# Even mixer: sixteen heads in two groups with one division each, weight splitting off GpSimd, the second group's keys moved behind three heads

## The chip, the core and the metric

The kernel runs on one core of one Trainium2 chip. The metric is the device time of one execution in microseconds (us), the median of several. The core has TensorE (PE, matrix products; the loading of its stationary side is shown as PEld), VectorE (DVE), ScalarE (ACT), GpSimd (POOL) and SyncE (SP), which here only issues DMAs. Each engine works through a queue of its own in a fixed order and waits on semaphores of the others.

## The reference

A decoder of two blocks on 256 tokens of width 1024 in fp32. The stages are, in order: a feed-forward layer, the even mixer, two feed-forward layers, the odd mixer, a feed-forward layer, and then the second block's mixer and feed-forward layer. The change lies in the even mixer, which computes

```python
proj = h @ w_in                                   # 1024 -> 1536
qa, ka, va, qb, kb, vb = split(proj)              # 8 + 2 + 2 heads of 64, twice
qa = apply_axial_rope(rms_norm(qa, q_gain)); ka = apply_axial_rope(rms_norm(ka, k_gain))
oa = softmax(qa ka^T / 8) va                      # 8 query heads, 2 key heads, all 256 keys
qb, kb = apply_rope(qb), apply_rope(kb)
ob = softmax with sink(qb kb^T / 8, |q - k| <= 128) vb
return concatenate([oa, ob]) @ w_out
```

## The kernel before, in words

Activations lie with the features on the 128 partitions. Weights are streamed from memory in blocks of 128 x 1024 (`load_unit`, line 254, five buffers) and split into a rounded part wh and a rest wl: `prep` (line 277) makes wh on ACT (line 288) and wl on DVE or, for the blocks that `ON_POOL` (line 117) names, on GpSimd (line 290). `block` (line 294) hands out the next block and first prepares all up to LOOK = 6 blocks ahead; wh and wl have five buffers each.

The program is traced once. A scheduler then fixes the order of each engine's queue from a model of the times: an instruction that was written earlier goes first, one that is ready may be put ahead of one that is not. Buffers come from pools by tag: NSLOT common slots of 128 x 1024, and for temporaries of 512 columns the tag c2 with seven buffers (`tmp`, line 232), which w2, p and pT share. PSUM has four banks mm, two sc for scores and two aux for transposes.

`mix0` (line 636) is the even mixer. FIRST is the windowed group of eight heads (b = 1), SECOND the global one (b = 0). The program goes:

1. `proj(kv)` (line 748): four weight blocks, PE lines 341 to 343, read out by ACT with the row scale of the norm (line 660).
2. `k_in(FIRST)`: rotation of the first group's keys (`rot`, line 678): a product t (line 687, mostly on GpSimd), two multiplies on DVE (line 693) and a sum (line 695).
3. `proj(q[FIRST])`, `q_in(FIRST)`: the queries and their rotation. `k_T(FIRST)`: transposes on PE (line 701) and copies to kp.
4. `k_in(SECOND)`: squares on GpSimd (line 667), sums on DVE (line 668), an inverse root (`rsqrt`, line 431: three ACT and four GpSimd steps), scaling (line 675), rotation. Then `q_T(FIRST)`, four transposes, and `k_T(SECOND)`, which clears the halves of kT on GpSimd (line 560) and splits the transposed keys (lines 553, 554).
5. `proj(q[SECOND])`, `q_in(SECOND)`.
6. Heads one after the other (`attention`, line 610): scores (lines 567 or 569), maximum with the mask on DVE (line 779), exponential with its sum on ACT (line 577), the sink's term (line 786), reciprocal (line 584) and scaling of p by it (line 587, one half on GpSimd, one on DVE); two heads later the transposes of p (line 594) and the copy pT (line 596); three heads later, for each pair of heads, the products with v (line 603, v loaded, pT moving, 256 columns) and the split into oh and ol (`split_tile`, line 606). Between the heads of FIRST stand the four `q_T(SECOND)` (lines 543, 544).
7. `out_half` 0 (line 1452) takes the four pairs of FIRST and is interleaved with the heads of SECOND step by step; `out_half` 1 follows.

The rows also show lines of the last mixer, `mix2`: its E tiles (line 1161), and the products of its softmax heads, with pT loaded and v moving, and their division (lines 1287 to 1300).

Of the kernel before, what the change touches and what calls it, by code (L numbers as in the profile page):

```python
# [10 lines left out]
F32R = mybir.dt.float32r  # L11
# [4 lines left out]
P = 128  # L16
T = 256
# [5 lines left out]
NSLOT = 23  # L23
# [93 lines left out]
ON_POOL = {"ffn2": (6, 16, 3), "mix0": (0, 20, 3), "mix1": (0, 32, 4)}  # L117
# [93 lines left out]
class K:  # L211
    def __init__(self, tc, ctx, aps, stages):
        self.tc, self.nc, self.aps, self.ctx = tc, tc.nc, aps, ctx
        pool = lambda n, b, **k: ctx.enter_context(tc.tile_pool(name=n, bufs=b, **k))
        self.cp = pool("const", 1)
        self.wp = pool("wp", 1)
        self.sp = pool("slots", 1)
        self.tp = pool("tmp", 1)
        self.ap_ = pool("att", 1)
        self.dp = pool("dram", 1, space=bass.MemoryType.DRAM)  # L220
        self.pp = pool("ps", 1, space=bass.MemoryType.PSUM)
        self.nblk = sum(STAGE_NBLK[s] for s in stages)
        self.raw, self.ready = {}, {}
        self.start = {s: sum(STAGE_NBLK[r] for r in stages[:i]) for i, s in enumerate(stages)}
        self.next_unit = self.next_prep = self.cur = 0
        self.n6 = 5

# [66 lines left out]
    def block(self):  # L294
        b = self.cur
        self.cur += 1
        while self.next_prep < min(self.nblk, b + LOOK):
            self.prep()
        return self.ready.pop(b)
# [336 lines left out]
    def mix0(self, next_gain):  # L636
# [25 lines left out]
        def rms(src, h, tagn, scale):  # L662

            ss = self.tmp("ss" + tagn, 2 * h, 1)
            for tt in range(2):
                sq = self.tmp("w2", 512, 2)[:, :h * 64]
                nc.gpsimd.tensor_tensor(out=sq, in0=src[:, tt], in1=src[:, tt], op=ALU.mult)
                nc.vector.tensor_reduce(out=ss[:, tt * h:(tt + 1) * h],
                                        in_=sq.rearrange("p (h d) -> p h d", d=64), axis=AX.X, op=ALU.add)
# [8 lines left out]
        def rot(src, dst, h, n, sub):  # L678

            for tt in range(2):  # L680
# [5 lines left out]
                e = nc.vector if (tt, n, h) == (1, 2, 8) else nc.gpsimd  # L686
                e.tensor_tensor(out=t3, in0=v, in1=C.unsqueeze(1).to_broadcast([P, h, 64]), op=ALU.mult)
# [21 lines left out]
        kT = [self.slot("kT", F32R).rearrange("p (n c) -> p n c", n=4)]  # L709
# [3 lines left out]
        self.zero_others(kp)  # L713
        qT = lambda b, t: qs[2 * b + t // 2][:, t % 2]
# [16 lines left out]
        def k_T(b):  # L731
            if b == FIRST:
                ps = tr(kr[:, b], 0)
                for h in range(2):
                    own = slice(64 * h, 64 * h + 64)
                    nc.scalar.activation(kp[own, h], ps[own], AF.Copy)
            else:
                self.zero_others(kT[b][:, 2:4])
                self.split_k(kT[b][:, 0:2], kT[b][:, 2:4], tr(kr[:, b], 0))
# [15 lines left out]
        k_in(SECOND)  # L755
        for t in range(4):
            q_T(FIRST, t)
        k_T(SECOND)
# [5 lines left out]

        def soft_a(i, ps):
            nm, den, mx = [self.tmp(n, 2, 3) for n in ("nm", "den", "mx")]
            r = rq[0][:, i:16:8]
            nc.vector.tensor_reduce(out=mx, in_=ps, axis=AX.X, op=ALU.max)
            nc.vector.scalar_tensor_tensor(out=nm, in0=mx, scalar=-1.0, in1=r, op0=ALU.mult, op1=ALU.mult)
            p = self.head_exp(ps, nm, den, [r[:, 0:1], r[:, 1:2]])  # L770
            self.head_norm(p, den)
            return p

        def soft_b(i, ps):
            nm, den = self.tmp("nm", 2, 3), self.tmp("den", 2, 3)
            mx, es = self.tmp("mx", 2, 3), self.tmp("es", 2, 3)
            s = ps
            for qt in range(2):
                nc.vector.tensor_tensor_reduce(out=s[:, qt], in0=ps[:, qt], in1=band[:, qt], scale=1.0,
                                               scalar=-3e38, op0=ALU.add, op1=ALU.max,  # L780
                                               accum_out=mx[:, qt:qt + 1])
            h = i
            nc.vector.tensor_scalar(out=nm, in0=mx, scalar1=-1.0, scalar2=nsink[:, h:h + 1],
                                    op0=ALU.mult, op1=ALU.min)
            p = self.head_exp(s, nm, den)
            nc.scalar.activation(es, nm, AF.Exp, bias=sink[:, h:h + 1])
            nc.vector.tensor_tensor(out=den, in0=den, in1=es, op=ALU.add)
            self.head_norm(p, den)
            return p

        def head(b, t, half):
            c = 128 + 256 * b + 64 * half
            v = [kv[:, kt, c:c + 64] for kt in range(2)]
            j = t if b == FIRST else 4 + t
            if b == FIRST:
                return lambda: (qp[:, t], kp, None, v, j, half)
            return lambda: (qT(b, t), kT[b][:, 0:2], kT[b][:, 2:4], v, j, half)

        def soft(i, ps):
            return (soft_b if (FIRST if i < 8 else SECOND) else soft_a)(i % 8, ps)  # L800

        hs = [head(b, t, half) for b in (FIRST, SECOND) for t in range(4) for half in range(2)]
        done = []
        att = self.attention(hs, soft, OH, OL, done)
        for _ in proj(q[SECOND]):
            pass
        q_in(SECOND)
# [719 lines left out]
```

## Time and profile before

| | |
|---|---|
| median of 3 runs | 1379.62 us (1379.5 to 1379.85) |
| the profiled execution | 1380.82 us, of which its span, first to last instruction, is 1379.0 |
| PE busy | 1327.5 us (96%) |
| DVE, ACT, GpSimd busy | 1012.8, 807.6 and 308.1 us |
| mean granted TensorE clock | 0.982 of 2.4 GHz |
| HBM read | 228.96 MB |
| even mixer | about 203.8 to 312.4 us of the span |

A granted clock of 1.00 means 2.4 GHz and one of 0.50 means 1.2 GHz. Matmuls are pipelined: a record is longer than the distance to the next one, so what a matmul costs is read from the starts of a series. An fp32 matmul that is not in the rounded form stands as two records. Idle time of an engine stands in brackets ahead of the instruction that ended it, with the one that released it.

### The profile page before, as it was taken

What the parts mean: (1) busy time and instruction counts of PE and PEld (TensorE: products, weight loads), DVE (VectorE), ACT (ScalarE), POOL (GpSimd) and SP (SyncE); (2) the same over time, 40 slices, a digit from 0 to 9 for tenths busy, and PEclk for the clock granted to TensorE, in tenths of its full rate; (3) what the DMA queues carried; (4) which work ended last, traced back from release to release, by engine and by line L of the source; (5) the groups of instructions that cost most, each with busy time, mean ns of one, the idle gap of its engine ahead of it and who ended that gap; (6) DMA issues with size and microseconds to landing.
All of it is one profiled execution on the core that took longest, in us unless ns stands there. A gap on an engine that the chain in (4) does not pass through costs nothing.

```text
span 1379.0 us, 22443 instructions
## 1 busy us (share of the span) xinstructions
PE 1327.5 (96%) x8150; PEld 1166.1 (85%) x8150; DVE 1012.8 (73%) x1841; ACT 807.6 (59%) x1496; POOL 308.1 (22%) x355
## 2 busy tenths in 40 slices
PE   6999999699999999999999999999999998999997
PEld 5888887488888888888899888888877888899987
DVE  7877666868776768776659878777767768787754
ACT  4655545656655446555468756555566546676642
POOL 4000146432000210001434340001243124641101
PEclk9999999899999999999999999999999998899999
DMA  7555555025555555555565345555545304265561
GB/s 255 184 184 189 190 196 173 32 77 183 185 192 189 183 177 191 190 192 183 184 229 193 113 167 185 183 190 192 184 141 186 118 33 152 92 199 181 184 216 47
DMA packets 64255, 231.48 MB, mean 168 GB/s; under 512 B 7240, under 2 KB 7376, under 8 KB 64144
## 3 DMA queue, kind: packets, MB, share of 16 engines
q1 hardware_dynamic: 61632, 221.41, 48.1%
q0 software_dynamic: 2512, 8.64, 1.8%
q8 instruction: 64, 1.05, 0.3%
q14 instruction: 47, 0.39, 0.1%
HBM read 228.96 MB, written 1.06 MB: 167 GB/s over the span
## 4 chain that ended last, share of the span: by engine, by line
PE 90%; DVE 6%; ACT 2%; issue 1%; DMA 0%; POOL 0%; DVEq 0%; SPq 0%; ACTq 0%
PE mm L308 25%; PE mm L306 14%; PE sc L308 7%; PE mm L312 5%; PE mm L313 5%; PE mm L314 5%; PE sc L306 4%; PE mm L343 4%; PE mm L341 4%; PE mm L342 4%; PE mm L305 3%; PE mm L603 2%; DVE wl L290 1%; PE sc L313 1%; PE sc L314 1%
## 5 line engine op out<-in xcount | busy, mean ns | idle before, releaser
L290 DVE TENSOR_TENSOR wl<-raw,wh 128x1024 fp32r<-128x1024 f32 (+1 forms) x406 | 502.4, 1240 | 267.7 <-ACT wh L288 266.5
L288 ACT ACTIVATE wh<-raw 128x1024 fp32r<-128x1024 f32 (+1 forms) x425 | 443.4, 1045 | 435.5 <-issue 201.8
L308 PE MATMUL mm<-xs,wh 128*128 128x512 f32 x826 | 297.7, 400 | 3.2 <-DVE xs L410 3.2
L306 PE MATMUL mm<-xs,wl 128*128 128x256 f32 x944 | 245.5, 281 | 0.0
L308 PE MATMUL mm<-h,wh 128*128 128x512 f32 x672 | 237.9, 398 | 0.0
L306 PE MATMUL mm<-h,wl 128*128 128x256 f32 x704 | 191.5, 280 | 0.0
L306 PEld LDWEIGHTS mm<-xs,wl 128*128 128x128 f32 x944 | 179.7, 190 | 10.6
L308 PEld LDWEIGHTS mm<-xs,wh 128*128 128x128 f32 x826 | 155.8, 189 | 36.9 <-DVE xs L410 5.4
L413 POOL TENSOR_TENSOR sq<-xt 128x256 f32<-128x256 f32 x48 | 41.1, 859 | 513.1 <-DVE xt L527 483.5
L308 PEld LDWEIGHTS mm<-h,wh 128*128 128x128 f32 x672 | 126.0, 188 | 29.2
L308 PE MATMUL sc<-xs,wh 128*128 128x512 f32 x406 | 144.8, 396 | 0.0
L306 PEld LDWEIGHTS mm<-h,wl 128*128 128x128 f32 x704 | 132.9, 189 | 3.1
L306 PE MATMUL sc<-xs,wl 128*128 128x256 f32 x464 | 120.1, 279 | 0.0
L312 PE MATMUL mm<-xs,wh 128*128 128x256 f32 x384 | 110.5, 289 | 1.0 <-ACT wh L288 0.8
L313 PE MATMUL mm<-xs,wh 128*128 128x256 f32 x384 | 110.2, 287 | 0.1
L314 PE MATMUL mm<-xs,wl 128*128 128x256 f32 x384 | 109.6, 286 | 0.3 <-DVE wl L290 0.3
L306 PEld LDWEIGHTS sc<-xs,wl 128*128 128x128 f32 x464 | 87.5, 188 | 5.1
L308 PEld LDWEIGHTS sc<-xs,wh 128*128 128x128 f32 x406 | 76.1, 188 | 15.5
L312 PEld LDWEIGHTS mm<-xs,wh 128*128 128x128 f32 x384 | 73.8, 193 | 3.6 <-issue 1.5
L313 PEld LDWEIGHTS mm<-xs,wh 128*128 128x128 f32 x384 | 74.0, 193 | 1.6 <-issue 0.8
L314 PEld LDWEIGHTS mm<-xs,wl 128*128 128x128 f32 x384 | 74.0, 193 | 1.3 <-issue 0.7
L343 PE MATMUL mm<-wh,xs 128*128 128x512 f32 x144 | 56.6, 397 | 1.6 <-DVE xs L959 1.6
(376 smaller groups left out, 2683.0 us busy)
## 6 DMA issues: line engine op xcount, KB each, us to landing
raw<-wst SPq DMA_DIRECT2D x417, 512.0 KB, 3.3
m1b<-m1bias POOLq DMA_DIRECT2D x8, 512.0 KB, 4.8
xt<-xT SPq DMA_DIRECT2D x4, 256.0 KB, 5.1
patf<-m2pat POOLq DMA_DIRECT2D x2, 512.0 KB, 6.5
kb<-scr POOLq DMA_DIRECT2D x2, 512.0 KB, 4.5
out<-x2n SPq DMA_DIRECT2D x4, 256.0 KB, 2.0
raw<-wst SPq DMA_DIRECT2D x2, 256.0 KB, 4.3
m0tab<-m0tab POOLq DMA_DIRECT2D x1, 512.0 KB, 4.6
```

The lines of the kernel that those rows point to most:

```text
L288: self.nc.scalar.activation(wh[:, c], r[:, c], AF.Copy)
L290: e.tensor_tensor(out=wl[:, c], in0=r[:, c], in1=wh[:, c].bitcast(F32), op=ALU.subtract)
L305: mm(ps, wh, x2, start=True, stop=False)
L306: mm(ps[:, :T], wl, x2[:, :T], start=False, stop=False, skip_group_check=True)
L308: mm(ps, wh, x2, start=False, stop=last)
L312: mm(ps, wh, xh, start=first, stop=False)
L313: mm(ps, wh, xl, start=False, stop=False)
L314: mm(ps, wl, xh, start=False, stop=last)
L341: mm(ps, xh, wh, start=first, stop=False)
L342: mm(ps, xh, wl, start=False, stop=False)
L343: mm(ps, xl, wh, start=False, stop=last)
L413: nc.gpsimd.tensor_tensor(out=sq, in0=self.x(j), in1=self.x(j), op=ALU.mult)
```

## The change

Weight blocks of this mixer are split by DVE alone. The squares of the rms norm go to ACT, the product t of every rotation to DVE. The second group's keys are prepared behind the first three heads of the first group instead of ahead of all heads, and the look-ahead of the weights is set to 1 while the second group's queries are projected. Each group of eight heads is one generator, `group`: it keeps the sums of all its heads in den, multiplies unscaled p with v in such a way that pT is loaded and v moves (64 columns), gathers all eight heads in two PSUM banks with the tokens on the partitions, divides once, transposes the result in four pieces and splits it. The second group's heads come from a second call, interleaved with the first output half as before. The rests of the split keys get a tile of their own, kT becomes a c2 temporary, a slot o holds each group's result, and NSLOT falls from 23 to 22.

```diff
-NSLOT = 23
+NSLOT = 22
-ON_POOL = {"ffn2": (6, 16, 3), "mix0": (0, 20, 3), "mix1": (0, 32, 4)}
+ON_POOL = {"ffn2": (6, 16, 3), "mix1": (0, 32, 4)}
...
-        while self.next_prep < min(self.nblk, b + LOOK):
+        while self.next_prep < min(self.nblk, b + self.look):
...
-                nc.gpsimd.tensor_tensor(out=sq, in0=src[:, tt], in1=src[:, tt], op=ALU.mult)
+                nc.scalar.activation(sq, src[:, tt], AF.Square)
...
-                e = nc.vector if (tt, n, h) == (1, 2, 8) else nc.gpsimd
-                e.tensor_tensor(out=t3, in0=v, in1=C.unsqueeze(1).to_broadcast([P, h, 64]), op=ALU.mult)
+                nc.vector.tensor_tensor(out=t3, in0=v, in1=C.unsqueeze(1).to_broadcast([P, h, 64]), op=ALU.mult)
...
-        kT = [self.slot("kT", F32R).rearrange("p (n c) -> p n c", n=4)]
+        kT = self.tmp("kT", 2 * T, dt=F32R).rearrange("p (n c) -> p n c", n=2)
...
+        kl = self.ap_.tile([P, 2, T], F32R, tag="klo", name="kl", bufs=1)
+        self.zero_others(kl)
...
-                self.zero_others(kT[b][:, 2:4])
-                self.split_k(kT[b][:, 0:2], kT[b][:, 2:4], tr(kr[:, b], 0))
+                self.split_k(kT, kl, tr(kr[:, b], 0))
...
         k_T(FIRST)
-        k_in(SECOND)
         for t in range(4):
             q_T(FIRST, t)
-        k_T(SECOND)
...
+        def group(b):
+            st = {}
+            po = [self.mm_ps().rearrange("p (h d) -> p h d", h=8) for _ in range(2)]
+            for i in range(8 + 3):
+                if i < 8:
...
+                    scale = (soft_b if b else soft_a)(i, ps)
+                    p = self.tmp("p", 2 * T).rearrange("p (a b) -> p a b", a=2)
+                    for qt in range(2):
+                        nc.scalar.activation(p[:, qt], ps[:, qt], AF.Exp, bias=nm[:, b, qt, i:i + 1],
+                                             scale=scale[qt] if scale else 1.0,
+                                             accum_out=den[:, b, qt, i:i + 1])
+                    st[i] = p
+                yield
+                j = i - 2
+                if 0 <= j < 8:
+                    st[j] = self.head_T(st[j])
+                j = i - 3
+                if 0 <= j < 8:
+                    pT = st.pop(j)
+                    c = 128 + 256 * b + 64 * (j % 2)
+                    for tt in range(2):
+                        for kt in range(2):
+                            nc.tensor.matmul(po[tt][:, j], pT[:, kt, tt * P:(tt + 1) * P], kv[:, kt, c:c + 64],
+                                             start=kt == 0, stop=kt == 1)
+                yield
...
+            rd = self.tmp("grd", 16, 2).rearrange("p (t h) -> p t h", t=2)
+            nc.vector.reciprocal(rd, d)
+            o = self.slot("o").rearrange("p (t c) -> p t c", t=2)
+            for tt in range(2):
+                nc.vector.tensor_tensor(out=o[:, tt].rearrange("p (h d) -> p h d", h=8), in0=po[tt], op=ALU.mult,
+                                        in1=rd[:, tt].unsqueeze(2).to_broadcast([P, 8, 64]))
+            for t in range(4):
+                j = t if b == FIRST else 4 + t
+                self.split_tile(OH(j), OL(j), tr(o, t * P))
+                yield
+
+        att = group(FIRST)
+        self.look = 1
         for _ in proj(q[SECOND]):
             pass
+        self.look = LOOK
+        for _ in range(6):
+            next(att)
+        k_in(SECOND)
+        k_T(SECOND)
         q_in(SECOND)
-        for _ in range(4):
-            next(att)
-        n = 0
-        while len(done) < 4:
+        for n, _ in enumerate(att):
             if n % 2 == 0 and n < 8:
                 q_T(SECOND, n // 2)
-            next(att)
-            n += 1
-        self.interleave(self.out_half(OH, OL, 0, None), att)
+        self.interleave(self.out_half(OH, OL, 0, None), group(SECOND))
```

## Rows read from the trace of the kernel before

**Rows 1.** Busy time of each engine by stretch of the even mixer (start and end in us, length, then busy us and number of instructions of PE, PE's weight loads, DVE, ACT and GpSimd, the granted clock of TensorE, the DMA share and GB/s). The first sum is that of 204 to 237.7, the last that of 237.9 to 312.4:

```profile
sum 33.70, PE 33.70 PEld 27.76 DVE 21.01 ACT 18.79 POOL 20.86; mean PE 11.23 PEld 9.25 DVE 7.00 ACT 6.26 POOL 6.95
...
243.20:256.80 13.60, 5.67 (x16) 4.01 (x17) 12.96 (x41) 6.50 (x24) 4.72 (x8) 0.50 0.15 49
...
sum 74.40, PE 61.94 PEld 48.30 DVE 57.28 ACT 46.00 POOL 33.24; mean PE 12.39 PEld 9.66 DVE 11.46 ACT 9.20 POOL 6.65
```

**Rows 2.** The chain of waits that set the end, the piece that holds the keys' rotation (start, us on the chain, what):

```profile
237.49 8.14 DVE kr L693 x4
```

**Rows 3.** The two kinds of multiply of line 693, by source line: shortest, median and longest in ns, first and last start in us:

```profile
L693 DVE TENSOR_TENSOR kr<-kv,m0g x8: 210/216/7814, 217.7 to 245.4; 128x64 f32<-128x64 f32 x8
L693 DVE TENSOR_TENSOR qr<-q,m0g x8: 408/412/1520, 226.3 to 248.8; 128x256 f32<-128x256 f32 x8
```

**Rows 4.** Timeline of GpSimd, 226 to 246 (start, us, line, operation; in brackets the idle time before it and what ended it):

```profile
226.36 1.54 POOL L687 TENSOR_TENSOR w<-q,m0g 128x512 f32<-128x512 f32 x1 [4.71 <-ACT q L660]
...
230.40 1.65 POOL L667 TENSOR_TENSOR w<-kv 128x128 f32<-128x128 f32 x2
...
237.66 0.87 POOL L687 TENSOR_TENSOR w<-kv,m0g 128x128 f32<-128x128 f32 x2
...
242.79 2.48 POOL L687 TENSOR_TENSOR w<-q,m0g 128x512 f32<-128x512 f32 x2
```

**Rows 5.** Timeline of PE, 236 to 272:

```profile
237.95 1.89 PE L567 MATMUL sc<-kp,qp 128*128 128x256 f32 x8
...
245.97 0.66 PE L701 MATMUL aux<-ident,kr 128*128 128x128 f32 x2 [5.92 <-DVE kr L695]
251.43 2.08 PE L567 MATMUL sc<-kp,qp 128*128 128x256 f32 x4 [4.80 <-ACT p L577]
...
258.77 0.66 PE L594 MATMUL aux<-ident,p 128*128 128x128 f32 x4
```

**Rows 6.** Timelines of GpSimd (the two DMA issues) and of ACT (the first write of the last xs slot):

```profile
16.52 0.59 POOL L268 DMA_DIRECT2D m0row<-m0row  x1
...
199.37 0.49 ACT L409 ACTIVATE xs<-xt,cols 128x256 fp32r<-128x256 f32 x1
...
199.78 0.58 POOL L268 DMA_DIRECT2D m0tab<-m0tab  x1
```

**Rows 7.** Timeline of DVE, 213 to 237.5:

```profile
217.65 1.18 DVE L693 TENSOR_TENSOR kr<-kv,m0g 128x64 f32<-128x64 f32 x4
218.75 0.48 DVE L695 TENSOR_TENSOR kr<-kr,w 128x128 f32<-128x128 f32 x2
...
232.70 0.69 DVE L695 TENSOR_TENSOR qr<-qr,w 128x512 f32<-128x512 f32 x1
...
234.45 0.47 DVE L668 TENSOR_REDUCE ssk<-w 128x2 f32<-128x128 f32 x2
...
236.99 0.49 DVE L675 TENSOR_TENSOR kv<-kv,rrk 128x128 f32<-128x128 f32 x2 [0.94 <-POOL rrk L442]
```

**Rows 8.** Groups of instructions from 200 to 320, shapes kept apart (count, busy us, mean ns, idle before):

```profile
L290 DVE TENSOR_TENSOR wl<-raw,wh 128x1024 fp32r<-128x1024 f32 x17 | 21.7, 1274 | 14.5 <-ACT wh L288 14.4
...
L577 ACT ACTIVATE p<-sc,nm 128x256 f32<-128x256 f32 x16 | 7.4, 468 | 3.4 <-DVE nm L783 2.9 <-DVE rd L584 0.5
...
L779 DVE CUSTOM_DVE_ANT_0 sc<-sc,m0tab 128x256 f32<-128x256 f32 x16 | 6.8, 423 | 0.6 <-PE sc L567 0.5
...
L544 DVE SCALAR_TENSOR_TENSOR qT<-aux,qT 64x256 fp32r<-64x256 f32 x8 | 3.4, 422 | 0.3
...
L779 DVE DVE_READ_ACCUMULATOR2_ANT mx<- 128x1 f32 x16 | 2.1, 134 | 0.0
...
L783 DVE TENSOR_SCALAR nm<-mx,nsink 128x2 f32<-128x2 f32 x8 | 1.8, 221 | 0.1
...
L668 DVE TENSOR_REDUCE ssq<-w 128x8 f32<-128x512 f32 x2 | 1.3, 668 | 0.0
```

**Rows 9.** Timeline of ACT in the last mixer, the second E tile of the third head and the last copy of the second head:

```profile
1092.79 1.08 ACT L1161 ACTIVATE E<-mm 128x512 f32<-128x512 f32 x2 [0.80 <-PE mm L1160]
...
1099.51 0.28 ACT L1198 ACTIVATE A<-aux 128x128 f32<-128x128 f32 x1 [1.23 <-PE aux L1197]
```

**Rows 10.** The chain of waits for the pairs' products (line 603) of today; timeline of PE for the same kind of product in the last mixer; by source line, DVE's division there:

```profile
297.29 1.01 PE mm L603 x6
...
298.89 0.57 PE mm L603 x2
...
1101.69 0.33 PE L1287 MATMUL mm<-va,pT 128*128 128x64 f32 x2
...
1102.29 0.48 PE L1159 MATMUL mm<-patr,lh 128*128 128x512 f32 x1
...
L1300 DVE TENSOR_TENSOR mix<-mm,frd x4: 414/416/425, 1112.0 to 1125.7; 128x256 f32<-128x256 f32 x4
```

**Rows 11.** Busy time by stretch, around two places where PE idles (columns as in rows 1):

```profile
993.00:1000.90 7.90, 5.37 (x41) 4.83 (x39) 4.50 (x8) 3.73 (x6) 1.59 (x2) 1.00 0.44 151
1000.90:1007.70 6.80, 6.80 (x33) 6.80 (x34) 2.35 (x4) 3.04 (x9) 1.39 (x7) 0.50 0.23 77
1018.00:1024.00 6.00, 4.40 (x23) 2.45 (x22) 6.00 (x8) 5.64 (x11) 6.00 (x7) 1.00 0.27 87
```

More of the change, by code (lines that the diff above doesn't have):

```diff
@@ L763, in mix0 @@
         OL = lambda t: ol[t // 4][:, (t % 4) * T:(t % 4 + 1) * T]
+        den, nm = [self.tmp(n, 32, 1).rearrange("p (g t h) -> p g t h", g=2, t=2) for n in ("gden", "gnm")]
         def soft_a(i, ps):
-            nm, den, mx = [self.tmp(n, 2, 3) for n in ("nm", "den", "mx")]
+            mx = self.tmp("mx", 2, 3)
             r = rq[0][:, i:16:8]
             nc.vector.tensor_reduce(out=mx, in_=ps, axis=AX.X, op=ALU.max)
-            nc.vector.scalar_tensor_tensor(out=nm, in0=mx, scalar=-1.0, in1=r, op0=ALU.mult, op1=ALU.mult)
@@ L770, in soft_a @@
-            p = self.head_exp(ps, nm, den, [r[:, 0:1], r[:, 1:2]])
-            self.head_norm(p, den)
-            return p
+            nc.vector.scalar_tensor_tensor(out=nm[:, 0, :, i], in0=mx, scalar=-1.0, in1=r,
+                                           op0=ALU.mult, op1=ALU.mult)
+            return [r[:, 0:1], r[:, 1:2]]
         def soft_b(i, ps):
-            nm, den = self.tmp("nm", 2, 3), self.tmp("den", 2, 3)
-            mx, es = self.tmp("mx", 2, 3), self.tmp("es", 2, 3)
-            s = ps
+            mx = self.tmp("mx", 2, 3)
@@ L778, in soft_b @@
             for qt in range(2):
-                nc.vector.tensor_tensor_reduce(out=s[:, qt], in0=ps[:, qt], in1=band[:, qt], scale=1.0,
+                nc.vector.tensor_tensor_reduce(out=ps[:, qt], in0=ps[:, qt], in1=band[:, qt], scale=1.0,
                                                scalar=-3e38, op0=ALU.add, op1=ALU.max,
                                                accum_out=mx[:, qt:qt + 1])
-            h = i
-            nc.vector.tensor_scalar(out=nm, in0=mx, scalar1=-1.0, scalar2=nsink[:, h:h + 1],
+            nc.vector.tensor_scalar(out=nm[:, 1, :, i], in0=mx, scalar1=-1.0, scalar2=nsink[:, i:i + 1],
@@ L784, in soft_b @@
                                     op0=ALU.mult, op1=ALU.min)
[L785 to L804, printed above, removed]
+            return None
+        def group(b):
[3 more added lines that the diff above has]
+                if i < 8:
+                    t, h = i // 2, i % 2
+                    if b == FIRST:
+                        ps = self.head_scores(qp[:, t], kp, None, h)
+                    else:
+                        ps = self.head_scores(qT(b, t), kT, kl, h)
+                    scale = (soft_b if b else soft_a)(i, ps)
[18 more added lines that the diff above has]
+                yield
+            d = den[:, b]
+            if b:
+                es = self.tmp("es", 16, 1).rearrange("p (t h) -> p t h", t=2)
+                nc.vector.tensor_tensor(out=es, in0=nm[:, b], in1=sink.unsqueeze(1).to_broadcast([P, 2, 8]),
+                                        op=ALU.add)
+                nc.scalar.activation(es, es, AF.Exp)
+                nc.vector.tensor_tensor(out=d, in0=d, in1=es, op=ALU.add)
+            rd = self.tmp("grd", 16, 2).rearrange("p (t h) -> p t h", t=2)
[8 more added lines that the diff above has]
+                yield
@@ L805, in mix0 @@
+        att = group(FIRST)
+        self.look = 1
         for _ in proj(q[SECOND]):
             pass
+        self.look = LOOK
+        for _ in range(6):
+            next(att)
+        k_in(SECOND)
+        k_T(SECOND)
         q_in(SECOND)
-        for _ in range(4):
-            next(att)
-        n = 0
-        while len(done) < 4:
+        for n, _ in enumerate(att):
             if n % 2 == 0 and n < 8:
                 q_T(SECOND, n // 2)
-            next(att)
-            n += 1
-        self.interleave(self.out_half(OH, OL, 0, None), att)
+        self.interleave(self.out_half(OH, OL, 0, None), group(SECOND))
```

## The prediction

> **What bounds the kernel now.** I read the page first: TensorE (PE) is busy for almost the whole span, so a change to the even mixer is worth only what it does to the few places where PE stands still. I then read busy time by stretch for this mixer [rows 1]. While the three projections run, PE has no idle time at all. The attention of the sixteen heads and the output projection take the 74.4 us from 237.9 to 312.4; of these PE is busy for 61.94, so it idles for 12.46. From 243.2 to 256.8 the granted clock is 0.50, the lower level of 1.2 GHz; the 5.67 us of PE work in there would have taken half as long at 2.4 GHz, so 2.8 us more are lost. In all 12.46 + 2.8 = 15.3 us can be won here, and no more, since the work itself stays.
>
> The chain of waits names the cause of the idle time: VectorE's (DVE) rotation of the second group's keys, 8.14 us of the path [rows 2]. By line, one such multiply takes 0.21 us and the worst 7.81 us [rows 3]. GpSimd works without a break from 237.66 to 245.27 on a weight block, the squares and the rotation's products [rows 4], and DVE's instruction ends as that run ends. On PE the keys' transposes come 5.92 us late, and the third head's scores 4.80 us after that [rows 5].
>
> **How the order around it comes about.** Each engine runs a fixed order that the scheduler made: earlier lines first where they are ready. The trace shows a second rule. The load of m0row, which has a buffer of its own, is issued at 16.52; the load of m0tab, which takes one of the common slots, waits until 199.78, right after the last of the four xs slots is first written at 199.37 [rows 6]. So buffers of one tag are given out in the order of their first use in the program. The temporaries of 512 columns (w2, p, pT, and now kT) share one tag too. GpSimd idles 4.71 us before 226.36 and squares the keys of kv at 230.40 only, though DVE rotates the other keys of the same kv from 217.65 [rows 4, 7]: their w2 stands behind that of the queries' rotation. I take it that this order holds for the new code.
>
> **The change part by part.** *Weight blocks off GpSimd, squares to ScalarE (ACT), products to DVE.* This ends the 7.81 us block. Seven weight blocks at 1.27 us, three 512-column products at 0.69 (as a sum of that shape) and four small ones at 0.24 come to DVE, some 12 us [rows 7, 8]. Ahead of 237.9 they are hidden: DVE is busy 21.0 of 33.7 us there, part of it blocked, and PE waits for nothing [rows 1]. If that cover were gone, a weight block would cost its 1.27.
>
> The Trainium skill (SBUF — State Buffer, Who interferes with whom) says that a DVE instruction with two SBUF inputs and a GpSimd one that reads SBUF exclude each other for a whole instruction. Row 7.81 against 0.21 us agrees; by that rule alone the change would give back about 7.6 us, to 1372.0. It says nothing of what is late next; its case is the faster rival below.
>
> *Keys of the second group behind three heads.* What is late next is their own chain. In program order p of heads 0 to 2 and pT of head 0 now take their buffers first, then the squares of the keys, the rotation's products, kT, the squares and products of the queries, and only then p of head 3. Scores start at 238.0. A head costs 0.95 on PE (1.89 for two), 1.25 on DVE (twice 0.42 + 0.13, less their overlap, and 0.22), 0.94 on ACT (two exponentials at 0.47) [rows 5, 8]. With two score banks the third head's scores wait for the first exponentials, 241.2, and its own end near 244.7. From there: two squares, 0.55 (0.28 for an ACT pass of 128x128); reduces 0.47; the inverse root, 2.07 from 234.92 to 236.99; scaling 0.49; rotation 1.58 and two products, 0.5; transposes and the first copy, 0.8: 251.1 [rows 7, 9]. Then the queries: two rotations of a product at 0.69, two multiplies at 0.41 and a sum at 0.69, 4.4 us, and transposes, 0.4: 255.9 at the least [rows 3, 7]. With the reduces (1.3), the keys' low parts (0.84, as the queries' at 0.42 each) and two heads' maxima (2.5) ahead of them on DVE it is 260.5 [rows 8]. I take 256.3, near the lower end, since DVE has waits of the chain in which to do those. Head 1's transposes stand behind these on PE, whose auxiliary banks are also one tag: 256.6. Today head 1's transposes come at 258.77 [rows 5]. In those 18.6 us PE has five heads' scores, one head's transposes (0.5) and products (0.9) and 0.8 of other transposes, 6.95 in all, so it idles 11.7, and the clock falls as it does today, 2.8. **New wait: +14.5**, against the 15.3 removed; bounds +2 (if the chain runs ahead of the heads) to +19. Who waits: all heads from the third on. The five later weight preparations (1.27 on DVE each) fall into this wait and cost nothing; without it they would be 6.4 us on DVE.
>
> *One division per group.* Per head the reciprocal, the sum and the scaling of p go. What PE still waits for them is in the 12.46 already. What is new is a tail after each group: nothing of oh exists before the last head's product. DVE divides two 128x512 pieces (0.42 for 256 columns [rows 10], so about 0.68 each), PE transposes and ACT copies, 0.8 as above; with the handoffs about 2.3 us. Behind the first group two heads' scores of the second (at most the 1.89 of the first group's) cover part, I take 1.3: **+1.0**, between 0 and 2.3. Behind the second group nothing covers it, because the first output half is interleaved one step to one with the heads and runs out before them; before the change the output half takes each pair as it comes. That is 2.3 us of idle PE. What the clock does then is open: after 2.53 us of idle PE between 993 and 1000.9 it was at 0.50 for 6.8 us, which costs 3.4; with 1.60 between 1018 and 1024 it stayed at 1.00 [rows 11]. I take the middle, 1.7: **+4.0**, between 1.5 and 5.7.
>
> [...]
>
> *Products with p as the loaded side.* Eight records for a head now have 128-column loads and 64 moving columns. The same form elsewhere goes at 0.11 each (0.60 for six), 0.88 a head; today a pair takes 1.01 + 0.57, 0.79 a head [rows 10]. Sixteen heads: **+1.4**. *Eight pairs of transposes of the outputs*, 0.25 each, two of them inside the tails: **+1.5**.
>
> *One slot less.* In the last mixer the second E tile of the third head is written at 1092.79 while, by my count of live tiles, all 23 slots are taken; the second head's E is free at about 1099.5 [rows 9]. With 22 that write comes up to 6.7 us later. The third head's work follows the second's on every engine anyway, so I take 0, between 0 and 4, something over half of the 6.7.
>
> **Sum.** -15.3 + 14.5 + 1.0 + 4.0 + 1.4 + 1.5 = +7.1. The profiled execution took 1380.82 (span 1379.0); I put the difference on the median of three runs, 1379.62: **1386.7**.
>
> **The rivals.** *The chain runs ahead of the heads, and it gets faster.* If buffers are not held to program order, DVE and ACT prepare the keys before 237.9. Then the first group is bound by DVE: eight heads at 1.25, the queries' rotation and reduces 5.7, their splitting 8 x 0.42, 19 us from 238 [rows 8], and 3 us behind it to the last product, plus the tail: 262.3. PE has 20.9 us of work in those 24.3, 3.4 idle, no slow clock: -15.3 + 3.4 + 4.0 + 1.4 + 1.5 = -5.0, **1374.6** (1372 to 1377). It decides from the point where head 3's exponentials start before about 250. For it: GpSimd is clear, and scores did move ahead of earlier lines on PE. Against it: the m0tab load and the late squares of the keys.
>
> *The new wait and the savings cancel.* The chain is partly hidden, head 3 starts around 252 and the last tail keeps its clock: the wait comes to +9 and that tail to +2.3, so -15.3 + 9 + 1.0 + 2.3 + 1.4 + 1.5 = -0.1, **1379.5** (1377 to 1382).
>
> *The missing slot bites.* On top of the forecast the third and fourth heads of the last mixer end late, and its output projection with them: up to +4, **1390.7**. Against it: only one tile of one head stands behind the slot.
>
> That the block of DVE goes on by other GpSimd work is no case of its own: only four small steps per inverse root, 0.2 each, remain.
>
> **How the numbers follow.** The forecast with its chain bounds has 0.44, the slot on top 0.08, the cancelling 0.18, the faster rival 0.30. A measurement of this kernel tells apart about 0.2%, 2.8 us: below 1376.9 is faster, above 1382.4 slower. The faster rival gives 0.27 to faster and 0.03 to same; the cancelling one 0.16 to same, 0.01 to each side; the forecast 0.43 to slower and 0.01 to same. So faster 0.28, same 0.20, slower 0.52. The range goes from the middle of the faster rival, 1374, to the upper bound of the chain and the slot, 1392; the likeliest case alone is 1382 to 1391.
>
> **What would show it.** Right: no DVE multiply over 1 us; head 3's exponentials near 254 or later, ACT's squares of the keys after the third head's exponentials; PE idle some 11 us between 245 and 257 at a clock of 0.50; a PE gap of about 2 us just before the second output half. Wrong: squares of the keys before 238, or the first group's last product before 266. The forecast falls with the chain: each microsecond that it is hidden takes one from the sum.

## The result, and the profile after

The changed kernel takes 1389.9 us (median of four runs, 1388.7 to 1391.4), the kernel before 1379.7 beside it: ratio 1.0072, interval 1.006 to 1.0084, slower by 10.2 us. The forecast was 1386.7 in a range of 1374 to 1392. The profiled execution after takes 1389.73, span 1388.0; the span before is 1379.0, so the two traces differ by 9.0.

Where do these 9.0 us come from? First the even mixer of the kernel after in four stretches (columns as in [rows 1]; the first begins with the first scores, the last ends with the first matmul of the next feed-forward layer):

```profile
237.22:251.44 14.22, 6.98 (x38) 5.44 (x36) 10.35 (x43) 7.07 (x24) 0.79 (x4) 1.00 0.23 76
251.44:265.10 13.66, 9.29 (x33) 7.06 (x32) 8.37 (x22) 8.06 (x24) 0.86 (x4) 0.50 0.00 0
265.10:296.00 30.90, 29.83 (x251) 29.00 (x252) 17.69 (x42) 20.87 (x61) 0.00 (x0) 1.00 0.15 52
296.00:317.32 21.32, 19.57 (x162) 18.72 (x161) 11.80 (x21) 10.75 (x23) 5.67 (x6) 1.00 0.15 51
sum 80.10, PE 65.68 PEld 60.21 DVE 48.21 ACT 46.75 POOL 7.33; mean PE 16.42 PEld 15.05 DVE 12.05 ACT 11.69 POOL 1.83
```

A stretch's length (the first number behind the times) less its busy PE is idle PE: 7.2, 4.4, 1.1 and 1.8 us, 14.4 in all. The second stretch runs at a clock of 0.50, which costs half of its 9.29, 4.6 us. What is left, 61.0 us, is PE's work at full clock. The same sum for the kernel before (first scores 237.95 to 312.19, 74.2 us) is 12.6 idle, 2.8 for the slow clock, 58.9 of work. So the cure of one wait was paid for by another of the same kind. PE's timeline shows where it stands (in brackets the idle time before an instruction and what ended it), to be held against [rows 5]:

```profile
242.04 0.44 PE L595 MATMUL aux<-ident,p 128*128 128x128 f32 x2 [2.72 <-ACT p L798]
...
246.16 1.13 PE L568 MATMUL sc<-kp,qp 128*128 128x256 f32 x4 [1.45 <-ACT p L798]
...
251.19 0.49 PE L701 MATMUL aux<-ident,kr 128*128 128x128 f32 x2 [3.06 <-DVE kr L695]
253.67 0.45 PE L701 MATMUL aux<-ident,qr 128*128 128x128 f32 x1 [1.99 <-DVE qr L695]
255.55 2.07 PE L568 MATMUL sc<-kp,qp 128*128 128x256 f32 x4 [1.43 <-ACT p L798]
```

Two gaps of 5.92 and 4.80 have become five of 1.4 to 3.1 us: first the maxima of the first heads, then the keys' rotation, then the queries', then the fourth head. ACT's timeline (start, us, line, operation) gives the order behind it:

```profile
245.56 0.46 ACT L798 ACTIVATE p<-sc,gnm 128x256 f32<-128x256 f32 x1
...
246.00 0.59 ACT L597 ACTIVATE pT<-aux 128x512 f32<-128x512 f32 x1
246.48 0.51 ACT L668 ACTIVATE w<-kv 128x128 f32<-128x128 f32 x2
...
252.50 1.15 ACT L668 ACTIVATE w<-q 128x512 f32<-128x512 f32 x2
...
254.47 0.47 ACT L798 ACTIVATE p<-sc,gnm 128x256 f32<-128x256 f32 x1
```

The squares of the second group's keys come after the third head's exponentials and the first head's pT, although kv was there by 217; the fourth head's exponentials ("head 3" of the prediction) start at 254.47. DVE's block is gone: by source line, its multiplies of the rotation are all of one length ([rows 3] had a longest of 7814 ns):

```profile
L693 DVE TENSOR_TENSOR kr<-kv,m0g x8: 216/218/222, 217.1 to 250.6; 128x64 f32<-128x64 f32 x8
L693 DVE TENSOR_TENSOR qr<-q,m0g x8: 416/418/426, 226.2 to 239.0; 128x256 f32<-128x256 f32 x8
```

The next layer starts 5.1 us later than before (317.32 against 312.19). Another 3.7 us arise in the last mixer and behind it. The heads of the last mixer, from PE's first use of an E tile to its last, take 63.2 us (1068.8 to 1132.0) against 60.4. By stretch (columns as above; the heads after, a slow stretch within them, the heads before):

```profile
1068.80:1132.00 63.20, 60.05 (x418) 52.87 (x417) 46.14 (x175) 31.56 (x87) 8.21 (x20) 0.97 0.23 76
1125.26:1128.67 3.41, 3.23 (x13) 2.94 (x14) 1.88 (x5) 0.83 (x3) 0.00 (x0) 0.50 0.00 0
```

```profile
1063.80:1124.20 60.40, 57.89 (x418) 51.27 (x417) 45.89 (x175) 31.89 (x87) 8.21 (x20) 1.00 0.24 79
```

Only 0.6 us of the difference is idle PE; 1.6 is the clock of 0.50, and the rest is a little more work of PE. The timeline of ACT shows what moved: the second E pair of the third head, at 1092.79 before [rows 9], is written 32.3 us after the first product, before it was 29.0:

```profile
1099.92 0.37 ACT L1298 ACTIVATE p<-sc,nm 128x128 f32<-128x128 f32 x1 [2.89 <-DVE nm L1294]
...
1101.10 1.09 ACT L1191 ACTIVATE E<-mm 128x512 f32<-128x512 f32 x2
```

It has moved behind a head's exponentials, and ACT stands idle for 2.89 us where the pair was written before. The last feed-forward layer is 1.0 longer, by a new gap of PE, 0.95 ahead of 1190.28.

### The profile page after: what moved, and what is told of

It reads as the page before. It is cut to its first block, busy times and chain, and to the rows that moved or that the text cites. A ratio compares the mean times of both kernels' runs of the same rounds, so it can differ in the third digit from the quotient of the medians.

```text
span 1388.0 us, 22501 instructions
## 1 busy us (share of the span) xinstructions
PE 1333.2 (96%) x8230; PEld 1178.6 (85%) x8230; DVE 1009.3 (73%) x1823; ACT 807.0 (58%) x1493; POOL 266.1 (19%) x321
## 4 chain that ended last, share of the span: by engine, by line
PE 91%; DVE 4%; ACT 3%; issue 1%; DMA 0%; POOL 0%; DVEq 0%; SPq 0%; ACTq 0%
PE mm L309 25%; PE mm L307 14%; PE sc L309 7%; PE mm L313 5%; PE mm L314 5%; PE mm L315 5%; PE mm L344 4%; PE mm L342 4%; PE mm L343 4%; PE sc L307 4%; PE mm L306 3%; PE sc L314 1%; PE sc L313 1%; PE sc L315 1%; PE aux L595 1%
## 5 line engine op out<-in xcount | busy, mean ns | idle before, releaser
L291 DVE TENSOR_TENSOR wl<-raw,wh 128x1024 fp32r<-128x1024 f32 (+1 forms) x413 | 513.9, 1247 | 260.8 <-ACT wh L289 259.5
L309 PE MATMUL mm<-h,wh 128*128 128x512 f32 x672 | 237.7, 397 | 0.0
L309 PEld LDWEIGHTS sc<-xs,wh 128*128 128x128 f32 x406 | 76.1, 188 | 15.6
```

The lines of the kernel that those rows point to most:

```text
L291: e.tensor_tensor(out=wl[:, c], in0=r[:, c], in1=wh[:, c].bitcast(F32), op=ALU.subtract)
L309: mm(ps, wh, x2, start=False, stop=last)
```

## The experiments

Every kernel was timed several times beside the kernel before. The table takes one profiled execution of each apart in the way shown above; times in us. "Even mixer" goes from the first scores to the next layer, "heads" are those of the last mixer, "last layer" is from the last matmul of the last mixer's output projection to the last matmul of all, and "slow" is what PE lost in the even mixer to the clock of 0.50.

| kernel | median | ratio, interval | even mixer | idle | slow | work | heads | last layer |
|---|---|---|---|---|---|---|---|---|
| before | 1379.7 | | 74.2 | 12.6 | 2.8 | 58.9 | 60.4 | 209.6 |
| after | 1389.9 | 1.0072 (1.0060 to 1.0084) | 80.1 | 14.4 | 4.6 | 61.0 | 63.2 | 210.7 |
| e1 before, 22 slots | 1383.3 | 1.0029 (1.0019 to 1.0039) | 74.3 | 12.6 | 2.8 | 58.9 | 63.2 | 210.7 |
| e2 after, 23 slots | 1385.5 | 1.0046 (1.0033 to 1.0059) | 80.2 | 13.9 | 5.2 | 61.0 | 60.5 | 209.5 |
| e3 before, GpSimd's work moved | 1374.0 | 0.9960 (0.9947 to 0.9972) | 67.5 | 7.4 | 1.5 | 58.6 | 60.4 | 209.8 |
| e4 after, keys ahead | 1385.0 | 1.0040 (1.0027 to 1.0052) | 73.1 | 8.6 | 3.4 | 61.0 | 63.2 | 210.6 |
| e5 after, keys' own tag | 1384.8 | 1.0042 (1.0029 to 1.0055) | 76.4 | 9.5 | 6.4 | 60.5 | 63.2 | 210.6 |
| e6 after, one head in front | 1384.2 | 1.0035 (1.0022 to 1.0047) | 76.9 | 12.7 | 3.7 | 60.5 | 63.0 | 210.0 |
| e7 e4 with 23 slots | 1377.8 | 0.9992 (0.9981 to 1.0003) | 72.2 | 9.1 | 1.7 | 61.3 | 60.4 | 209.9 |
| e8 e3, blocks held back | 1382.3 | 1.0018 (1.0010 to 1.0027) | 69.0 | 7.4 | 3.3 | 58.3 | 60.3 | 215.9 |
| e9 e7, blocks not held back | 1376.7 | 0.9984 (0.9972 to 0.9997) | 73.1 | 8.9 | 3.4 | 60.8 | 60.5 | 209.8 |
| e10 e3, heads before queries | 1375.8 | 0.9976 (0.9966 to 0.9985) | 68.7 | 6.3 | 2.9 | 59.4 | 60.4 | 209.4 |
| e11 before, weight blocks moved only | 1384.0 | 1.0034 (1.0021 to 1.0047) | 69.8 | 9.1 | 1.9 | 58.8 | 60.3 | 217.8 |
| e12 e3, keys behind three heads | 1384.1 | 1.0046 (1.0032 to 1.0061) | 76.1 | 9.5 | 8.2 | 58.4 | 60.3 | 215.0 |

Read the stage columns first: the medians also hold the last layer and the slow stretches of other stages, of which more below. And the profiled execution need not be a middle one: in e2, e5 and e6 it took 2.4, 3.6 and 4.0 us more than the median, in e1, e3 and e7 1.9, 1.7 and 2.1 less.

**e1, the missing slot in the kernel before.**

```diff
-NSLOT = 23
+NSLOT = 22
```

> The kernel before with 22 slots in place of 23, nothing else changed; the whole computation is there. Theory (the missing slot is what the last mixer loses): the second E tile of the third head, written at 1092.79 in the kernel before, comes about 3.5 us later, behind the third head's exponentials, and the kernel is slower by 3 to 5 us: about 1383.7. The offset of the last mixer is then the slot's alone. Rival (the last mixer's loss comes from the shift of the even mixer or from another order of the weights, not from the slot): 1379.7, within 0.5 us, and that E tile stays near 1092.8.

Slower by 0.29%, 3.4 us between the two medians (1383.25 against 1379.84), and the even mixer is the same to 0.1. The heads of the last mixer are as long as in the changed kernel. On this kernel's own clock the E pair stands at 1092.80, but its first product with E was at 1060.5 (before: 1063.8), so it is again 32.3 us after it:

```profile
1091.62 0.37 ACT L1268 ACTIVATE p<-sc,nm 128x128 f32<-128x128 f32 x1 [2.90 <-DVE nm L1264]
...
1092.80 1.09 ACT L1161 ACTIVATE E<-mm 128x512 f32<-128x512 f32 x2
```

The row by itself would have spoken for the rival; positions must be taken from the stage's start. The slot is the cause. Part of its price is the clock: in the traces of all five kernels with 22 slots the heads hold a slow stretch of 3.41 us, which costs 1.6 to 1.7, and in those of the nine with 23 slots none.

**e2, the slot given back.**

```diff
-NSLOT = 22
+NSLOT = 23
-        kl = self.ap_.tile([P, 2, T], F32R, tag="klo", name="kl", bufs=1)
+        kl = self.ap_.tile([P, 2, T], F32R, tag="kl0", name="kl", bufs=1)
```

> The changed kernel with its 23rd slot back; room for it comes from letting the low part of the keys (kl) share its 2 KB with a tile that the odd mixer uses later. Theory of the slot: the last mixer is as long as before the change, so 1389.9 less about 4: 1386 (1385 to 1387), and no half clock near 1125. Rival: the same 1389.9 within 0.7, with the half clock near 1125 still there.

1385.5, 4.4 less than the changed kernel; heads 60.5 and last layer 209.5 as before the change, and no slow clock in the heads. E1 and e2 give the slot much the same price from both sides, 3.4 and 4.4 us.

**e3, GpSimd's work alone.**

```diff
-ON_POOL = {"ffn2": (6, 16, 3), "mix0": (0, 20, 3), "mix1": (0, 32, 4)}
+ON_POOL = {"ffn2": (6, 16, 3), "mix1": (0, 32, 4)}
-                nc.gpsimd.tensor_tensor(out=sq, in0=src[:, tt], in1=src[:, tt], op=ALU.mult)
+                nc.scalar.activation(sq, src[:, tt], AF.Square)
-                e = nc.vector if (tt, n, h) == (1, 2, 8) else nc.gpsimd
-                e.tensor_tensor(out=t3, in0=v, in1=C.unsqueeze(1).to_broadcast([P, h, 64]), op=ALU.mult)
+                nc.vector.tensor_tensor(out=t3, in0=v, in1=C.unsqueeze(1).to_broadcast([P, h, 64]), op=ALU.mult)
```

> The kernel before with one part of the change alone: no weight block on GpSimd in the even mixer, its squares on ScalarE, its rotation products on VectorE. Theory (the 7.81 us multiply was a block by GpSimd's work, and its removal is worth nearly all of the 15.3 us of idle PE and half clock): PE gaps of 5.92 and 4.80 shrink to 2 to 3 in all, the clock stays at 1.00, and the time is 1379.7 less 9 to 12: about 1369. Rival (VectorE then has some 12 us more work and is late by itself, as the weight blocks fall between the rotations): gain of 3 us or less, 1377 or more, with PE gaps of 8 us or more before 257.

The even mixer is 6.7 us shorter, the time 5.9 less: the best kernel of the study, faster than both. It lies between the two expectations. The block is gone (by source line; line 692 here is the multiply of line 693), but one gap stays on PE (its timeline):

```profile
L692 DVE TENSOR_TENSOR kr<-kv,m0g x8: 215/216/218, 217.1 to 235.8; 128x64 f32<-128x64 f32 x8
```

```profile
244.76 1.92 PE L567 MATMUL sc<-kp,qp 128*128 128x256 f32 x4 [4.35 <-ACT p L577]
```

In this gap DVE does a weight block (1.23), two 512-column products, two multiplies and a reduce before the last step to the first head's maximum, nm, at 243.43, for which ACT waits. That is the work taken from GpSimd and the queries' rotation, so the 15.3 us could not all be had in this way.

**e4 and e5, two ways to let the keys go first.** In e4 the code is moved:

```diff
+        k_in(SECOND)
+        k_T(SECOND)
         att = group(FIRST)
...
-        k_in(SECOND)
-        k_T(SECOND)
         q_in(SECOND)
```

> The changed kernel with the second group's keys (k_in and k_T of SECOND) back ahead of the second query projection, where the kernel before has them; everything else as in the changed kernel, 22 slots. Theory (the keys' chain stands behind the first three heads by the order in which buffers of one tag are handed out, and the heads from the third on wait for it): squares of the keys before 230, head 3's exponentials at 250 or earlier against 254.47, PE idle between 243 and 257 down from 9 to 4 us or less, little or no half clock: 1389.9 less 5 to 9, about 1383. Rival (VectorE and ScalarE set the pace of the first heads anyway, through the query rotation and the weight block at 240): a gain of under 2 us, 1388 or more.

In e5 the code stays where the change put it; the keys' small temporaries alone, those of both groups, take buffers of another tag:

```diff
-                sq = self.tmp("w2", 512, 2)[:, :h * 64]
+                sq = (self.tmp("w2", 512, 2)[:, :h * 64] if h == 8 else self.tmp("w2k", 128, 2))
```

(the same for the product t in rot, and kl in tag kl0 to make room).

> The changed kernel, its program order and 22 slots kept, but the 128-column squares and products of the keys (w2 in k_in of SECOND) take buffers of a tag of their own (1 KB) in place of the common 512-column tag; room comes from the shared kl. Theory (the keys wait for p of the first three heads only because they stand behind it in one tag): squares and rotation of the keys run before 238 although the program still has them behind three heads; head 3's exponentials at 251 or earlier against 254.47; a gain like that of moving the code, 4 to 5.5 us: about 1385. Rival (it is the place in the program, and the tag is beside the point): squares at 246.5 as in the changed kernel, 1389.9 within 1.

Both medians are 5 us lower (1385.0, 1384.8). In e5 the squares run at 219.2, 27 us earlier than in the changed kernel, with the three heads still ahead of them in the program:

```profile
L668 ACT ACTIVATE w2k<-kv x2: 292/294/295, 219.2 to 219.4; 128x128 f32<-128x128 f32 x2
```

In e4 they run at 229.1. The fourth head's exponentials (timeline of ACT in e4) start there at 251.31, in e5 at 251.47, 3 us earlier than in the changed kernel and 0.5 to 1.3 later than expected:

```profile
248.85 1.16 ACT L668 ACTIVATE w<-q 128x512 f32<-128x512 f32 x2
...
251.31 0.47 ACT L798 ACTIVATE p<-sc,gnm 128x256 f32<-128x256 f32 x1 [1.30 <-DVE gnm L780]
```

PE's idle time falls by 5.8 and 4.9. So the place in the program held the keys back only through the order of the tag's buffers; e5 is the direct proof. That the heads gain no more than 3 us lies with DVE, by e4's trace: after the keys are out of the way the queries' products, multiplies and reduces stand there, and ACT waits for a maximum.

**e6, one head in front in place of three.**

```diff
-        for _ in range(6):
+        for _ in range(2):
             next(att)
```

> The changed kernel with one head of the first group in front of the second group's keys and queries in place of three (2 steps for 6). Theory (the chain starts when p of the last head in front has its buffer): squares of the keys right behind the exponentials of the first head, near 242 to 243.5 in place of 246.48, the later heads about 3 us earlier: a gain of 1.5 to 3.5 us, 1386.4 to 1388.4. Rival (heads 1 and 2 now stand behind the whole chain in their turn, so that the wait only changes its place): 1389.9 within 1, with a PE gap of 5 us or more before the second head's products.

The squares follow the first head's exponentials at once (timeline of ACT):

```profile
243.09 0.46 ACT L798 ACTIVATE p<-sc,gnm 128x256 f32<-128x256 f32 x1
...
243.54 0.50 ACT L668 ACTIVATE w<-kv 128x128 f32<-128x128 f32 x2
```

With three heads it was 246.48 behind the third: the chain starts when p of the last head in front has its buffer. The even mixer is 3.2 us shorter and the median 5.7 lower. Idle PE falls by only 1.8: gaps of 3.01 (keys) and 2.00 (queries) are still there, 2.3 to 2.5 us earlier. That much fits the theory. The other 2.5 us of the median cannot be read from this trace: its execution took 1388.2, 4.0 above the median of the seven and only 1.5 less than the changed kernel's.

**e7 and e9, both repairs at once.** e7 is e4 with e2's two lines; e9 also drops `self.look = 1`, so that weight blocks are prepared during the second query projection again.

> The changed kernel with both repairs at once: keys ahead of the second query projection, and 23 slots. Theory (the two losses are separate, one in the even and one in the last mixer): 1389.9 - 4.9 - 4.4 = 1380.6 (1379 to 1382), which leaves the products with p loaded, the transposes of the outputs and the tails, some 3 to 4 us, against the 5.9 that taking work off GpSimd alone gave. Rival (the two overlap, as both only change where the slow clock falls): 1383 or more.

> The changed kernel with keys ahead, 23 slots and weight blocks prepared during the second query projection as before (look of six blocks): what is left of the change is GpSimd's work moved, and one division per group with p as the loaded side. Against the run with GpSimd's work moved alone (1373.97, even mixer 67.5 long) it is the price of the division. Theory (prediction's terms: products 1.4, transposes of the outputs 1.5 as PE work, tails 1.5 to 2 as measured behind the groups): 4 to 5 us more, 1378 to 1379, work of PE up by 2.5 to 3 and idle by 1 to 2. Rival (the deferred blocks, not the division, make up the difference to that run; they stand on VectorE at 239 to 241 ahead of the first heads' maxima): 1374 to 1376.

e7: 1377.8, 12.1 less than the changed kernel where the two gains add up to 9.3 (4.9 + 4.4); the two losses are separate. The rest, 2.8, is no more than the slow stretches told of below can make: over the whole profile they cost 12.7 us here and 20.3 in the changed kernel. e9: 1376.7, whose interval overlaps that of e7, so holding the blocks back is worth nothing that can be measured. e9 differs from e3 by the division per group, and by which heads stand ahead of the queries. In the profiles its even mixer is 5.6 longer: work +2.2, idle +1.5, slow clock +1.8; between the medians it is 2.7. The sign is clear, the size is 2.7 to 5.6.

**e8, blocks held back in e3; e10, two heads ahead of the queries in e3.**

```diff
+        self.look = 1
         for _ in proj(q[SECOND]):
             pass
+        self.look = LOOK
```

> The kernel before with GpSimd's work moved as in the run that did that part alone (1373.97), and with no weight block prepared during the second query projection (the look of one block, as in the changed kernel); one division per head, keys ahead, 23 slots. Theory (the PE gap of 4.35 at 240.4 that was left there is VectorE's: a weight block of 1.2 us at 239.1 and one at 236.3 lie ahead of the first heads' maxima): the gap shrinks by 1 to 2 us and the time to 1372 to 1373. Rival (the gap is the chain of the queries of the second group on VectorE, and the held-back blocks only come later, between the heads): no gain, 1374 to 1376.

```diff
-        q_in(SECOND)
         for _ in range(4):
             next(att)
+        q_in(SECOND)
...
-            if n % 2 == 0 and n < 8:
-                q_T(SECOND, n // 2)
+            if n in (4, 6, 8, 10):
+                q_T(SECOND, n // 2 - 2)
```

> The kernel before with GpSimd's work moved (1373.97) and two heads of the first group ahead of the second group's queries (q_in), whose transposes are spread over heads four to seven; keys stay ahead, one division per head, 23 slots. Theory (the gap of 4.35 at 240.4 is VectorE doing the queries' rotation and reduces ahead of the first head's maxima; the heads do not need the queries until the ninth): the gap falls to 2 us or less, no half clock, 1371 to 1372.5. Rival (the queries' chain, started later, then holds the ninth head and the gap moves to 255 to 262): 1374 to 1376.

In e8 the gap of 4.35 became 3.18 + 1.25: no gain, as the rival said. Yet the kernel is 8.3 us slower than e3, and 6.1 of that are in the last feed-forward layer, which the edit does not touch. There DVE does two weight blocks in 5.05 us while GpSimd does one and the product before it (timelines of DVE and GpSimd):

```profile
1206.23 2.63 DVE L1375 SCALAR_TENSOR_TENSOR sg<-dv,cols,sg 128x254 f32<-128x254 f32 x1
...
1209.12 5.05 DVE L291 TENSOR_TENSOR wl<-raw,wh 128x1024 fp32r<-128x1024 f32 x2
```

```profile
1209.01 0.79 POOL L1380 TENSOR_TENSOR hp<-s,sg 128x256 f32<-128x256 f32 x1 [0.43 <-DVE sg L1375]
1209.75 3.34 POOL L291 TENSOR_TENSOR wl<-raw,wh 128x1024 fp32r<-128x1024 f32 x1
```

PE then stands for 4.45 us, and from 1215.28 to 1218.70 its clock is at 0.50 (PE's timeline):

```profile
1215.50 0.55 PE L313 MATMUL mm<-xs,wh 128*128 128x256 f32 x1 [4.45 <-DVE s L1375]
```

This is the block of [rows 2, 4] again, in another place. e11 and e12 have the same order there and the same 5.05; the other kernels do not. e10 shrank the gap to 2.56 and idle PE to 6.3, but lost 1.4 more to the slow clock: 1375.8, no better than e3. The time is the rival's, its reason is not: no gap over 0.84 stands between 255 and 265. The theory's gap and clock were not reached either.

**e11, the weight blocks alone; e12, the order alone.** e11 is the first two lines of e3's diff. e12 is e3 with the change's order: k_in and k_T of SECOND and q_in behind six steps of the heads.

> The kernel before with only the weight blocks of the even mixer taken off GpSimd; its squares and the products of the rotation stay there. It tells which part of GpSimd's work made VectorE's block. Theory (any long run of GpSimd blocks VectorE's two-input instructions; the run of 237.66 to 245.27 was a weight block, squares and products in turn): the block becomes shorter by the weight block's share, a rotation multiply of 3 us or more remains, and the time is between: 1375.5 to 1378. Rival (the weight block alone was the block): as good as with all of it moved, 1373 to 1375, no rotation multiply over 1 us.

> The kernel before with GpSimd's work moved (1373.97; even mixer 67.5 long) and, of the rest of the change, only the order: keys and queries of the second group behind three heads of the first; one division per head, 23 slots. Theory (the order alone makes the new wait, whatever the division): squares of the keys behind the third head's exponentials, even mixer 72 to 76 long, time 1379 to 1382. Rival (the wait needs the division per group too, whose p stays unscaled and whose maxima pass through one common tile): 1374 to 1376.

The multiplies of line 693 and GpSimd's products of the queries in e11 (by source line, then GpSimd's timeline):

```profile
L693 DVE TENSOR_TENSOR kr<-kv,m0g x8: 210/348/501, 218.0 to 237.5; 128x64 f32<-128x64 f32 x8
L693 DVE TENSOR_TENSOR qr<-q,m0g x8: 411/418/1522, 226.8 to 245.3; 128x256 f32<-128x256 f32 x8
```

```profile
241.62 3.47 POOL L687 TENSOR_TENSOR w<-q,m0g 128x512 f32<-128x512 f32 x2
```

e11: 4.5 us are gone from the even mixer, of e3's 6.7; the multiply of 7.81 is gone with the weight blocks alone, and the longest is 1.52, not 3 or more. But GpSimd's two 512-column products still take 3.47, and PE has a gap of 5.64 from 241.31 on, where e3 has 4.35. The weight block made the long multiply. The squares and products left on GpSimd go with the other 2.2 us; which of the two costs what was not tried apart. The median is above before because the last layer is 8.2 longer, in the way of e8. e12: the even mixer is 76.1, 8.6 longer than in e3, and that with one division per head. The squares of the keys come behind the third head again (timeline of ACT):

```profile
246.26 0.47 ACT L577 ACTIVATE p<-sc,nm 128x256 f32<-128x256 f32 x1
...
247.53 0.50 ACT L667 ACTIVATE w<-kv 128x128 f32<-128x128 f32 x2
```

The order alone makes the new wait. Of the 8.6 us, though, 2.1 are idle PE and 6.6 the clock, with slow stretches of 6.83 and 13.65 us, and what a wait costs in clock varies, as the last section shows. That the median is 10.1 above e3's includes 5.2 of the last layer, as in e8.

## Why the prediction came out as it did

The forecast was on the right side for the reason given. Its sum, term by term:

- *What can be won, 15.3*: 12.6 + 2.8 = 15.4. That GpSimd's run was the cause is shown by e3 (no multiply of the keys over 0.22 us, mixer 6.7 shorter) and divided in part by e11. The Trainium skill (SBUF — State Buffer, Who interferes with whom) says that a DVE instruction with two SBUF inputs contends with a GpSimd instruction that reads SBUF. The traces agree: such a multiply took 7.81 us beside GpSimd's run and 0.22 at most without it. The prediction drew 7.6 us from this rule alone; e3, which leaves the order of the keys as it was, gave 6.7 in the mixer.
- *New wait, +14.5*: 11.6 us of idle PE from 237.22 to 265.10 (10.7 of it from 238.0 to 256.6, the 18.6 us over which the forecast counted), against 11.7 forecast, and 4.6 for the clock against 2.8, 16.2 in all. The slow stretch is as long as before, 13.66 us, but it begins 8.3 us later: the forecast let it fall into the wait, where PE has 5.67 us of work; it fell behind most of it, onto 9.29. The cause, buffers of one tag in the order of first use, is shown by e5 and e6, and by e12 without the division. Head 3's exponentials start at 254.47, put at 254 or later, and head 1's transposes at 257.63, put at 256.6. The sign that PE idles 11 us between 245 and 257 was wrong in its place: the wait began at 239.3, with the queries' multiplies and a weight block on DVE ahead of the last step to the first head's maximum.
- *Tail behind the first group, +1.0*: nothing. The second group's scores at 276.02 cover it; the first output matmul starts at 277.77.
- *Tail behind the second group, +4.0*: 1.8 us of idle PE with all small gaps from 296 on, 0.9 of it in the tail itself, and no slow clock. DVE begins the division at 303.09, while PE's last products end at 303.50. So the gap of about 2 us that was to be a sign of being right did not show. The middle taken for the clock, 1.7, was a toss: e2, e4, e5, e7 and e9, with the same tail, have a slow stretch of 3.41 us behind it, the changed kernel and e6 have none. The first tail has no slow stretch behind it in any of the seven kernels that have it.
- *Products and transposes, 1.4 + 1.5*: 2.2 more of PE work.
- *One slot less, 0*: this is the term that was mis-sized. It is 2.7 in the heads and 1.0 in the last layer, 3.7, within the bound of 4 given; e1 and e2 show it alone. The reason for taking 0, that the third head's work follows the second's on every engine anyway, left out that each engine's order is made with the slot's wait in it: ACT writes the pair behind another head's exponentials and idles for 2.89 us, and 1.6 of the 2.7 is the clock of 0.50, of which the term had nothing. The mechanism was named as a rival, with a chance of 0.08, at 1390.7.

The sum from the trace: -15.4 + 14.4 idle + 4.6 slow + 2.2 work = 5.9 in the even mixer, of which 0.7 is an earlier first score, so 5.1 at the next layer; with 3.7 for the slot 8.8 of the 9.0 between the spans. The tails were put 3.2 us too high and the work 0.7, the new wait 1.7 too low and the slot 3.7; 1.1 of small gaps from 265 to 296 and the first score's 0.7 had no term. The parts cancel in part, which is luck, and the total is off by 1.9 between the spans and 3.1 between the medians. It is the case of the forecast with the slot's rival on top and smaller tails.

## What to carry to other kernels

Before a piece of code is moved behind another, look for the buffers that the two share: here a temporary of the keys, handed out in program order, tied a chain that was ready at 217 to the exponentials of 246, and a tag of its own undid that without moving a line. A buffer taken from a common pool for one stage must be priced in every other stage that fills the pool. And a change of several parts is best run in parts: the one part that took work off GpSimd would have given 5.9 us, where the whole cost 10.2.

## What the runs showed of the hardware

The same idle PE does not cost the same. Ahead of the last mixer PE has a gap of 2.08 or 2.09 us in every kernel (996.51 in the kernel before). The slow stretch that goes with it lasted 3.41 us (e1, e7, e9, e12), 6.83 (before, after, e3, e4, e8, e11) or 10.24 (e2, e5, e6, e10), all of it at 0.50:

```profile
1005.79:1012.62 6.83, 6.83 (x34) 6.83 (x34) 2.11 (x4) 3.19 (x9) 1.39 (x7) 0.50 0.21 78
```

```profile
1000.93:1004.34 3.41, 3.41 (x18) 3.41 (x17) 1.19 (x2) 1.40 (x5) 1.01 (x5) 0.50 0.38 112
```

```profile
992.50:1002.74 10.24, 9.99 (x45) 9.70 (x46) 3.32 (x6) 4.72 (x10) 2.74 (x9) 0.50 0.20 69
```

(after, e1 and e10, by stretch). At half of PE's busy time that is 1.7 to 5.0 us for one and the same wait, though the gap ahead of it is the same. One order holds in all fourteen traces: the later the stretch begins, the shorter it is. Beginnings from 0.17 us before the end of the gap to 0.02 behind it went with 10.24 us, from 0.25 to 2.31 behind it with 6.83, and from 2.45 to 3.05 with 3.41. Why it begins when it does was not tried and stays open, as does the exact price of the division. The runs of one kernel spread over 2 to 8 us; by the estimate from these three lengths (5.0 less 1.7) a forecast of a kernel like this carries some 3 us of it whatever its working.
